# Neighbourhood attention with stationary values: two heads in two column halves of the array, and the reciprocals transposed into the bank of the products

## The chip, the cores and the metric

The kernel runs on one core of one Trainium2 chip. The metric is the device time of one execution in microseconds (us). The profile and the trace come from one further execution that the hardware profiler recorded. Engines are PE (TensorE, the matrix array; PEld is its weight load), DVE (VectorE), ACT (ScalarE), POOL (GpSimd) and SP (which issues DMAs).

## The reference

One step of a two-layer network over 128 context tokens and 512 latent tokens, 640 in all, width 1024. The change lies in layer 1, in its attention alone. Cut to that:

```python
def context_attention(q, k, v):              # the 128 context tokens, 8 heads of 64
    s = jnp.einsum('bhqd,bhkd->bhqk', qi, k) * scale
    p = jax.nn.softmax(s, axis=-1)
    return jnp.einsum('bhqk,bhkd->bhqd', p, v)

def neighbourhood_attention(q, k, v, k_ctx, v_ctx, rpb):   # 512 latent tokens on an 8 x 64 grid
    ...
    s_loc = jnp.einsum('bhrcqd,bhrcyxd->bhrcqyx', qg, k_blk) * scale + bias
    s_ctx = jnp.einsum('bhrcqd,bhld->bhrcql', qg, k_ctx) * scale
    s = jnp.concatenate([s_loc.reshape(b, h, rows, ncb, Q_COLS, n_loc), s_ctx], axis=-1)
    p = jax.nn.softmax(s, axis=-1)
    out = (jnp.einsum('bhrcqyx,bhrcyxd->bhrcqd', p_loc, v_blk)
           + jnp.einsum('bhrcql,bhld->bhrcqd', p[..., n_loc:], v_ctx))
    return out.reshape(b, h, t, dh)
```

The output of the attention, together with that of a recurrent layer (S5) on other columns, goes through one projection. Around it stand normalisations, a 4096-wide squared-ReLU MLP per layer, and in layer 0 a pooling and convolution mixer.

## The kernel before

Activations lie transposed: features on the partitions, the 640 tokens along the free dimension. Nearly all of the time is matrix products of 128 x 128 weights against 320 tokens at a time, in three products each (high part and low part of both operands), from one helper line, L304. Instructions are issued in the order in which the Python code runs; the framework adds the semaphores and hands out the buffers. Each engine works through its own queue in that order, so an instruction that waits holds up everything behind it on its engine.

Attention (`attention`, a generator) has 20 steps: 4 pairs of heads `j`, and for each the query blocks `cb` = 0 to 4 of 128 queries. Blocks 0 to 3 are latent ones and see 384 keys (256 local, 128 of the context cache); block 4 is the context block and sees 128. In step `i` the generator issues, in this order, work for four different steps:

- `scores(i + 2)`: on PE the scores of both heads, each head on its own 64 rows of the array (L1391);
- `softmax(i + 2)`: on DVE the bias is added (L1399) and the maximum taken (L1401);
- `pv(i)`: on PE the value products (L1437) into a PSUM bank `bk`, then on DVE a multiplication by the reciprocal of the softmax sum into a tile `o` in SBUF (L1440);
- `trans(i + 1)`: on DVE the reciprocal (L1413); on PE `out(i - 1)`, the transposition of the finished `o` (L1445), then the transpositions of the exponentials `P` (L1419), all into one PSUM tile `pp`; on ACT the copy of the transposed `P` to `pT` (L1422), and `keep(i - 1)`, which writes the finished output as a high part (ACT, L453) and a low part (DVE, L454), both by the helper `two`;
- `expo(i + 2)`: on ACT the exponentials of the two heads with their sums (L1408).

PSUM has two kinds of buffers: three of the tiles `pp` (two banks each, `self.ps()`), and two single banks `bk` (`self.bank()`), which are handed out in turn. A buffer's next user waits until every reader of its last content is done.

`layer1` strews other work between the steps. Before steps 0, 2, 5, 7, 10 and 12 there is a projection `qk` of 48 products (L304, some 7 us of PE) whose result ACT copies to `xq` (L1113) before it splits the next weights (`wh`, L266). After steps 8, 16, 18 and 19 there is `s5_out`, 48 smaller products of the S5 layer (L1502, L1504), which ACT copies to `yp` (L1510) and sends out by a DMA that it issues itself. After steps 6, 9, 11 and 13 ACT and DVE turn parts of the S5 state round (`s5_turn`, L1484 and L1485), and before each `qk` DVE has a piece of the S5 scan in its queue (`scan_pump`).

Elsewhere in the program one line already has the form that the change brings in: L999 (the kernel matrices of S5) loads 64 columns of weights and streams 144 columns, twice side by side, into partitions 0 to 63 and 64 to 127 of one bank.

Of the kernel before, what the change touches and what calls it, by code (L numbers as in the profile page):

```python
# [6 lines left out]
F32 = mybir.dt.float32  # L7
F32R = mybir.dt.float32r
AF = mybir.ActivationFunctionType
# [196 lines left out]
class Net:  # L206
# [1151 lines left out]
    def attention(self):  # L1358
        nc = self.nc
        todo = [(j, cb) for j in range(4) for cb in (0, 1, 2, 3, 4)]  # L1360
        N = len(todo)
        st, bms = {}, {}
        self.rel_load(0)
        self.nb = self.nm = 0
        tok = lambda cb: slice(0, 128) if cb == 4 else slice(128 + 128 * cb, 256 + 128 * cb)

        def bias_ahead():
            while self.nb < min(N, self.nm + 2):
                if todo[self.nb][1] < 4:
                    bms[self.nb] = self.att_bias(*todo[self.nb])  # L1370
                self.nb += 1

        self.bias_ahead = bias_ahead
        yield

        def scores(i):
            j, cb = todo[i]
            if cb == 0 and j < 3:
                self.rel_load(j + 1)
            pt = self.ps()  # L1380
            q, k = self.q[j % 2], self.k[j % 2]
            if cb == 4:
                ks, w = [(0, k[:, 0:128])], 128
            else:
                g = 128 + 64 * (0, 1, 3, 4)[cb]
                ks, w = [(0, k[:, g:g + 256]), (256, self.ck[:, j])], 384
            for h in range(2):
                r = slice(64 * h, 64 * (h + 1))
                for o, kk in ks:
                    kk = kk[r]  # L1390
                    nc.tensor.matmul(pt[:, h, o:o + kk.shape[-1]], q[r, tok(cb)], kk, start=True, stop=True)  # L1391
            st[i] = [pt, w]

        def softmax(i):
            j, cb = todo[i]
            pt, w = st[i]
            self.nm += 1
            if cb < 4:
                nc.vector.tensor_add(pt[:, :, 0:256], pt[:, :, 0:256], bms.pop(i))  # L1399
            sm = self.tmp.tile([128, 3, 2], F32, name="sm", tag="sm", bufs=4)  # L1400
            nc.vector.tensor_reduce(sm[:, 0], pt[:, :, 0:w], axis=AX, op=OP.max, negate=True)  # L1401
            st[i].append(sm)

        def expo(i):
            pt, w, sm = st[i]
            P = self.tmp.tile([128, 2, 384], F32, name="P", tag="pa")
            for h in range(2):
                nc.scalar.activation(P[:, h, :w], pt[:, h, :w], AF.Exp, bias=sm[:, 0, h:h + 1], accum_out=sm[:, 1, h:h + 1])  # L1408
            st[i] = [P, sm, w]

        def trans(i):
            P, sm, w = st[i]
            nc.vector.reciprocal(sm[:, 2], sm[:, 1])  # L1413
            pt = self.ps()
            if i > 1:
                out(i - 2, pt[:, 0, 384:512])
            for h in range(2):
                for b in range(w // 128):
                    nc.tensor.transpose(pt[:, h, 128 * b:128 * (b + 1)], P[:, h, 128 * b:128 * (b + 1)], self.ident)  # L1419
            pT = self.t3("pT", 768).rearrange("p (h k) -> p h k", h=2)  # L1420
            for h in range(2):
                nc.scalar.activation(pT[:, h, :w], pt[:, h, :w], AF.Copy)  # L1422
            if i > 1:
                keep(i - 2)
            st[i][0] = pT

        def pv(i):
            j, cb = todo[i]
            pT, sm, w = st[i]
            po = self.bank()  # L1430
            vt, mix = self.vt, self.mix
            vs = ([vt[:, 1], vt[:, 2], self.cv], [mix[0], mix[1], self.cv], [mix[1], mix[2], self.cv],
                  [vt[:, 3], vt[:, 4], self.cv], [vt[:, 0]])[cb]
            for h in range(2):
                hs = slice(64 * (2 * j + h), 64 * (2 * j + h + 1))
                for b, vv in enumerate(vs):
                    nc.tensor.matmul(po[:, 64 * h:64 * (h + 1)], pT[:, h, 128 * b:128 * (b + 1)], vv[:, hs],  # L1437
                                     start=b == 0, stop=b == len(vs) - 1)
            o = self.tmp.tile([128, 2, 64], F32, name="o", tag="o")
            nc.vector.tensor_mul(o, po[:, 0:128].rearrange("p (h d) -> p h d", h=2),  # L1440
                                 sm[:, 2, :, None].to_broadcast([128, 2, 64]))
            st[i] = o

        def out(i, p):
            nc.tensor.transpose(p, st[i].rearrange("p h d -> p (h d)"), self.ident)  # L1445
            st[i] = p

        def keep(i):
            j, cb = todo[i]
            self.two(st.pop(i), *(a[:, tok(cb)] for a in self.os[j]))  # L1450

        bias_ahead()
        for i in range(2):
            scores(i)
            softmax(i)
        expo(0)
        expo(1)
        yield
        trans(0)
        for i in range(N):  # L1460
            bias_ahead()
            if i + 2 < N:
                scores(i + 2)
            if i + 2 < N:
                softmax(i + 2)
            pv(i)
            if i + 1 < N:
                trans(i + 1)
            if i + 2 < N:
                expo(i + 2)  # L1470
            if i == N - 1:
                for n in (i - 1, i):
                    out(n, self.bank()[:, 0:128])
                    keep(n)
            yield

    def s5_turn(self, q):
# [116 lines left out]
```

## Time and profile before

| what | value |
|---|---|
| time of three runs, median (lowest to highest) | 1484.7 us (1480.81 to 1505.91) |
| the profiled execution: its time | 1483.03 us |
| its span in the trace | 1481.3 us |
| mean granted clock of PE over the span | 0.987 |
| PE busy, share of the span | 96% |
| DVE, ACT, POOL busy | 60%, 33%, 40% |

The span begins with the first instruction and ends with the last; 1.7 us lie outside it. Busy shares are averages over stages with different limits. The attention steps with all that is strewn between them take the stretch from 812.5 to 936.5 us of the span.

### The profile page before, as it was taken

What the parts mean: (1) busy time and instruction counts of PE and PEld (TensorE: products, weight loads), DVE (VectorE), ACT (ScalarE), POOL (GpSimd) and SP (SyncE); (2) the same over time, 40 slices, a digit from 0 to 9 for tenths busy, and PEclk for the clock granted to TensorE, in tenths of its full rate; (3) what the DMA queues carried; (4) which work ended last, traced back from release to release, by engine and by line L of the source; (5) the groups of instructions that cost most, each with busy time, mean ns of one, the idle gap of its engine ahead of it and who ended that gap; (6) DMA issues with size and microseconds to landing.
All of it is one profiled execution on the core that took longest, in us unless ns stands there. A gap on an engine that the chain in (4) does not pass through costs nothing.

```text
span 1481.3 us, 24120 instructions
## 1 busy us (share of the span) xinstructions
PE 1428.6 (96%) x9757; PEld 1397.0 (94%) x9757; DVE 882.5 (60%) x1618; ACT 484.7 (33%) x856; POOL 587.8 (40%) x429
## 2 busy tenths in 40 slices
PE   7999999999999999999989999999999999999997
PEld 7999899999999999999988888998999999999996
DVE  7899986889988888844539764427541211211213
ACT  4321234312423432433433445535322312311321
POOL 2333021326788679734324321050433333333341
PEclk9999999999999999999999999999999999999998
DMA  9245531514544545524673323521532222222211
GB/s 377 86 174 175 185 129 59 186 57 142 194 173 152 176 169 175 178 83 155 224 219 127 99 80 101 201 72 58 169 116 72 72 86 72 72 81 76 73 58 71
DMA packets 73966, 193.30 MB, mean 131 GB/s; under 512 B 15360, under 2 KB 23936, under 8 KB 73344
## 3 DMA queue, kind: packets, MB, share of 16 engines
q1 hardware_dynamic: 68976, 188.99, 37.8%
q10 hardware_dynamic: 4880, 2.78, 0.6%
q8 instruction: 77, 1.26, 0.4%
q14 instruction: 33, 0.27, 0.1%
HBM read 170.51 MB, written 22.54 MB: 130 GB/s over the span
## 4 chain that ended last, share of the span: by engine, by line
PE 73%; DVE 13%; issue 5%; ACT 3%; POOL 2%; DMA 2%; SPq 0%; ACTq 0%; DVEq 0%; POOLq 0%
PE pp L304 64%; DVE condb L335 3%; PE bk L1437 2%; DVE wl L271 1%; PE pp L1319 1%; DVE x L449 1%; PE pp L1504 1%; PE bk L1242 1%; DVE hl L443 1%; PE pp L1419 1%; ACT wh L266 1%; PE pp L1391 1%; DMA raw<-wts 1%; PE bk L999 1%; DVE pb L681 1%
## 5 line engine op out<-in xcount | busy, mean ns | idle before, releaser
L273 POOL TENSOR_TENSOR wl<-raw,wh 128x1024 fp32r<-128x1024 f32 x112 | 277.3, 2480 | 605.2 <-ACT wh L266 545.0
L304 PE MATMUL pp<-hh,wl 128*128 128x320 f32 x1472 | 360.6, 316 | 9.7 <-ACT hh L437 6.3
L304 PE MATMUL pp<-hl,wh 128*128 128x320 f32 x1472 | 355.4, 312 | 2.2 <-DVE hl L636 2.0
L304 PE MATMUL pp<-hh,wh 128*128 128x320 f32 x1472 | 354.3, 311 | 0.0
L266 ACT ACTIVATE wh<-raw 128x1024 fp32r<-128x1024 f32 x178 | 186.3, 1051 | 327.3 <-PE pp L304 234.0
L304 PE MATMUL pp<-dh,wl 128*128 128x320 f32 x1152 | 280.1, 310 | 5.6 <-DVE x L449 2.7
L304 PE MATMUL pp<-dh,wh 128*128 128x320 f32 x1152 | 278.0, 309 | 0.0
L304 PE MATMUL pp<-dl,wh 128*128 128x320 f32 x1152 | 278.0, 309 | 0.0
L304 PEld LDWEIGHTS pp<-hh,wl 128*128 128x128 f32 x1472 | 251.9, 190 | 14.1 <-ACT hh L437 7.0
L304 PEld LDWEIGHTS pp<-hl,wh 128*128 128x128 f32 x1472 | 252.9, 190 | 3.7 <-DVE hl L636 2.8
L304 PEld LDWEIGHTS pp<-hh,wh 128*128 128x128 f32 x1472 | 253.0, 190 | 0.0
L449 DVE SCALAR_TENSOR_TENSOR x<-pp,mod,x 128x128 f32<-128x128 f32 (+2 forms) x240 | 91.5, 433 | 241.6 <-PE pp L304 241.3
L304 PEld LDWEIGHTS pp<-dh,wl 128*128 128x128 f32 x1152 | 195.9, 188 | 8.8 <-issue 5.6
L304 PEld LDWEIGHTS pp<-dl,wh 128*128 128x128 f32 x1152 | 196.6, 188 | 0.3 <-DVE dl L454 0.3
L304 PEld LDWEIGHTS pp<-dh,wh 128*128 128x128 f32 x1152 | 196.5, 188 | 0.0
L335 DVE SCALAR_TENSOR_TENSOR condb<-ada,condb 128x1024 bf16<-128x1024 f32 x124 | 182.7, 1474 | 2.4
L775 DVE SCALAR_TENSOR_TENSOR pp<-pp,t 128x640 f32<-128x640 f32 x64 | 53.1, 830 | 179.9 <-ACT t L774 179.9
L774 ACT ACTIVATE t<-pp 128x640 f32<-128x640 f32 x64 | 45.1, 704 | 253.4 <-PE pp L304 238.5
L392 POOL TENSOR_TENSOR acc<-acc,sq 128x320 f32<-128x320 f32 (+1 forms) x36 | 40.0, 1112 | 129.6 <-ACT sq L391 121.4
L271 DVE TENSOR_TENSOR wl<-raw,wh 128x1024 fp32r<-128x1024 f32 x66 | 90.0, 1363 | 0.0
L391 ACT ACTIVATE sq<-x 128x320 f32<-128x320 f32 (+1 forms) x51 | 29.1, 570 | 113.4 <-DVE x L449 107.0
L777 DVE TENSOR_TENSOR dl<-pp,dh 128x640 fp32r<-128x640 f32 x64 | 52.6, 822 | 3.9 <-DVE pp L775 0.5
(249 smaller groups left out, 1601.2 us busy)
## 6 DMA issues: line engine op xcount, KB each, us to landing
raw<-wts SPq DMA_DIRECT2D x178, 512.0 KB, 3.5
ada<-ada SPq DMA_DIRECT2D x80, 512.0 KB, 4.4
spare<-ada SPq DMA_DIRECT2D x16, 512.0 KB, 3.5
est<-s5e SPq DMA_DIRECT2D x16, 256.0 KB, 4.6
fst<-s5fc SPq DMA_DIRECT2D x16, 256.0 KB, 4.5
et<-est SPq DMA_DIRECT2D x16, 256.0 KB, 3.7
ft<-fst SPq DMA_DIRECT2D x8, 512.0 KB, 4.1
x<-x SPq DMA_DIRECT2D x8, 320.0 KB, 5.2
```

Source lines behind the costliest of these rows:

```text
L266: self.nc.scalar.activation(wh, raw, AF.Copy)
L271: self.defer(lambda: self.nc.vector.tensor_sub(wl, raw, wh.bitcast(F32)))
L273: self.nc.gpsimd.tensor_sub(wl, raw, wh.bitcast(F32))
L304: self.nc.tensor.matmul(o, a[:, w], b[:, s], start=first and n == 0, stop=last and n == 2)
L335: self.nc.vector.scalar_tensor_tensor(self.junk, a, 1.0, self.condb[:, c], op0=OP.mult, op1=OP.mult, accum_out=self.mod[:, l, j, f, c:c + 1])
L391: self.nc.scalar.activation(q, self.x[f][:, s], AF.Square)
L392: (self.nc.vector if f >= last else self.nc.gpsimd).tensor_add(self.acc[:, s], self.acc[:, s], q)
L449: self.nc.vector.scalar_tensor_tensor(self.x[f][:, s], p[:, s.start - 320 * h:s.stop - 320 * h], self.mod[:, l, j, f, c:c + 1], self.x[f][ ...
L774: self.nc.scalar.activation(t, p, AF.Relu)
L775: self.nc.vector.scalar_tensor_tensor(p, p, 0.0, t, op0=OP.max, op1=OP.mult)
L777: self.defer(lambda: self.nc.vector.tensor_sub(dl, p, dh.bitcast(F32)))
L1437: nc.tensor.matmul(po[:, 64 * h:64 * (h + 1)], pT[:, h, 128 * b:128 * (b + 1)], vv[:, hs], start=b == 0, stop=b == len(vs) - 1)
```

## The change

The value products swap their operands. Before, the transposed exponentials `pT` (128 keys x 128 queries) were the weights and 64 columns of values were streamed; the result had queries on the partitions. Now 64 columns of values are the weights and the 128 columns of `pT` are streamed; the result has the head's features on the partitions, head 0 in 0 to 63 and head 1 in 64 to 127, already transposed, so `out` and its transposition are gone. The reciprocals must then lie along the free dimension: DVE spreads them over 64 columns per head into a tile `r`, PE transposes `r` into columns 256 to 383 of the bank that takes the products, ACT copies that to `rt` in SBUF, and DVE multiplies the products by `rt` into columns 128 to 255 of the same bank. `keep` reads its source there, and now stands after `expo` at the end of the step; step `i` still keeps step `i - 1`.

```diff
@@ trans(i)
             nc.vector.reciprocal(sm[:, 2], sm[:, 1])
+            r = self.tmp.tile([128, 2, 64], F32, name="r", tag="o")
+            nc.vector.tensor_copy(r, sm[:, 2, :, None].to_broadcast([128, 2, 64]))
             pt = self.ps()
-            if i > 1:
-                out(i - 2, pt[:, 0, 384:512])
...
-            if i > 1:
-                keep(i - 2)
-            st[i][0] = pT
+            st[i][:2] = pT, r
@@ pv(i)
-            for h in range(2):
-                hs = slice(64 * (2 * j + h), 64 * (2 * j + h + 1))
-                for b, vv in enumerate(vs):
-                    nc.tensor.matmul(po[:, 64 * h:64 * (h + 1)], pT[:, h, 128 * b:128 * (b + 1)], vv[:, hs],
-                                     start=b == 0, stop=b == len(vs) - 1)
-            o = self.tmp.tile([128, 2, 64], F32, name="o", tag="o")
-            nc.vector.tensor_mul(o, po[:, 0:128].rearrange("p (h d) -> p h d", h=2),
-                                 sm[:, 2, :, None].to_broadcast([128, 2, 64]))
+
+            nc.tensor.transpose(po[:, 256:384], r.rearrange("p h d -> p (h d)"), self.ident)
+            rt = self.tmp.tile([128, 128], F32, name="rt", tag="rt")
+            nc.scalar.activation(rt, po[:, 256:384], AF.Copy)
+            for b, vv in enumerate(vs):
+                for h in range(2):
+                    hs = slice(64 * h, 64 * (h + 1))
+                    nc.tensor.matmul(po[hs, 0:128], vv[:, 128 * j + 64 * h:128 * j + 64 * (h + 1)],
+                                     pT[:, h, 128 * b:128 * (b + 1)], start=b == 0, stop=b == len(vs) - 1)
+            o = po[:, 128:256]
+            nc.vector.tensor_mul(o, po[:, 0:128], rt)
             st[i] = o
-
-        def out(i, p):
-            nc.tensor.transpose(p, st[i].rearrange("p h d -> p (h d)"), self.ident)
-            st[i] = p
@@ the loop over the steps
                 trans(i + 1)
             if i + 2 < N:
                 expo(i + 2)
+            if i:
+                keep(i - 1)
             if i == N - 1:
-                for n in (i - 1, i):
-                    out(n, self.bank()[:, 0:128])
-                    keep(n)
+                keep(i)
```

On PE, step 6 (the second of the two steps between two projections) stood before as follows; a row is the line, the operation, out<-in by tile names and the shape of the result, with the engines that it waits for in brackets.

```order
L1391 MATMUL pp<-attc,xq 128x128
L1437 MATMUL bk<-mix_8004,pT 128x64 [waits Activation_49]
L1437 MATMUL bk<-mix_8005,pT 128x64
L1437 MATMUL bk<-attc,pT 128x64
L1437 MATMUL bk<-mix_8004,pT 128x64 [waits Activation_49]
L1437 MATMUL bk<-mix_8005,pT 128x64
L1437 MATMUL bk<-attc,pT 128x64
L1445 MATMUL pp<-const,o 128x128 [waits DVE_49]
L1419 MATMUL pp<-const,P 128x128 [waits Activation_49]
```

The same place now:

```order
L1391 MATMUL pp<-attc,xq 128x128
L1433 MATMUL bk<-const,r 128x128 [waits DVE_49]
L1439 MATMUL bk<-pT,mix_8004 64x128 [waits Activation_49]
L1439 MATMUL bk<-pT,mix_8004 64x128
L1439 MATMUL bk<-pT,mix_8005 64x128 x2
L1439 MATMUL bk<-pT,attc 64x128 x2
L1419 MATMUL pp<-const,P 128x128 [waits PE_49]
```

The transposition of the reciprocals has moved in ahead of the value products, with a wait for DVE, and the transposition of `o` behind them is gone. In the built program the DVE instruction that L1433 waits for in step `i` is the low part (L454) of step `i - 2`, the last reader of that bank's former content, and the ACT instruction that the first L1439 waits for is the copy to `rt` out of the same bank (L1435 of the changed file).

On ACT, between two projections (steps 5 and 6), there stood before:

```order
L1113 ACTIVATE xq<-pp 128x640
L266 ACTIVATE wh<-raw 128x1024
L1422 ACTIVATE pT<-pp 128x384 x2
L453 ACTIVATE o_8031<-pp 128x128
L1408 ACTIVATE P,sm<-pp,sm 128x384 x2
L1422 ACTIVATE pT<-pp 128x384 x2
L453 ACTIVATE o_8031<-pp 128x128
L1408 ACTIVATE P,sm<-pp,sm 128x384 x2
```

And now:

```order
L1113 ACTIVATE xq<-pp 128x640
L266 ACTIVATE wh<-raw 128x1024
L1435 ACTIVATE rt<-bk 128x128
L1422 ACTIVATE pT<-pp 128x384 x2
L1408 ACTIVATE P,sm<-pp,sm 128x384 x2
L453 ACTIVATE o_8031<-bk 128x128
L1435 ACTIVATE rt<-bk 128x128
L1422 ACTIVATE pT<-pp 128x384 x2
L1408 ACTIVATE P,sm<-pp,sm 128x384 x2
L453 ACTIVATE o_8031<-bk 128x128
```

The copy to `rt` stands behind the weight split and ahead of the copies to `pT`; the high part of the finished output (L453) has moved behind the exponentials.

## Rows read from the trace of the kernel before

**Rows 1.** Windows: busy us (instructions) per engine, PEclk, DMA share, GB/s; the attention.
```profile
812.50:936.50 124.00, 115.08 (x895) 107.23 (x893) 72.86 (x162) 57.04 (x163) 27.05 (x30) 0.97 0.34 101
```

**Rows 2.** Timeline of PE, steps 5 and 6: start us, us, engine, line, operation.
```profile
846.79 0.71 PE L1391 MATMUL pp<-xq 64*128 64x256 f32 x4
...
847.65 0.66 PE L1437 MATMUL bk<-vt,pT 128*128 128x64 f32 x4
...
849.16 0.82 PE L1419 MATMUL pp<-const,P 128*128 128x128 f32 x6
849.91 0.71 PE L1391 MATMUL pp<-xq 64*128 64x256 f32 x4
...
852.84 0.54 PE L304 MATMUL pp<-hh,wl 128*128 128x320 f32 x2
```

**Rows 3.** Timeline of ACT and DVE in the same stretch.
```profile
846.90 0.70 ACT L1113 ACTIVATE xq<-pp 128x640 f32<-128x640 f32 x1 [4.89 <-PE pp L304]
847.50 1.05 ACT L266 ACTIVATE wh<-raw 128x1024 fp32r<-128x1024 f32 x1
...
850.01 0.87 ACT L1422 ACTIVATE pT<-pp 128x384 f32<-128x384 f32 x2 [1.46 <-PE pp L1419]
...
850.77 0.28 ACT L453 ACTIVATE o<-pp 128x128 fp32r<-128x128 f32 x1
850.93 0.59 ACT L1408 ACTIVATE P<-pp,sm 128x384 f32<-128x384 f32 x1
851.09 0.29 DVE L454 TENSOR_TENSOR o<-pp,o 128x128 fp32r<-128x128 f32 x1 [1.28 <-ACT o L453]
...
851.95 0.23 ACT L1408 ACTIVATION_READ_ACCUMULATOR P<-pp,sm 128x1 f32 x1
```

**Rows 4.** Timeline of PE at one block of L999, and the projection behind it.
```profile
378.30 0.71 PE L999 MATMUL bk<-s5f,bd 128*64 128x144 f32 x8
378.94 0.56 PE L304 MATMUL pp<-hh,wl 128*128 128x320 f32 x2
...
379.63 0.46 PE L304 MATMUL pp<-hl,wh 128*128 128x320 f32 x2
```

**Rows 5.** Timeline around ACT's copy `yp` behind step 8.
```profile
870.89 0.70 ACT L1510 ACTIVATE yp<-pp 128x640 f32<-128x640 f32 x1 [3.52 <-PE pp L1504]
871.63 0.38 ACTq L1511 DMA_DIRECT2D yds<-yp  x1
```

**Rows 6.** Timeline of ACT behind step 13: `s5_turn`.
```profile
905.60 1.57 ACT L1484 ACTIVATE tn<-S 64x128 f32<-64x128 f32 x4
```

**Rows 7.** Timeline of DVE and PE around steps 0 and 1.
```profile
815.26 0.66 PE L1437 MATMUL bk<-vt,pT 128*128 128x64 f32 x4 [1.08 <-ACT pT L1422]
...
819.85 0.15 DVE L1413 RECIPROCAL sm<-sm 128x2 f32<-128x2 f32 x1
...
821.93 0.30 PE L1445 MATMUL pp<-const,o 128*128 128x128 f32 x1 [2.12 <-DVE sm L1413]
...
823.27 0.54 PE L304 MATMUL pp<-hh,wl 128*128 128x320 f32 x2
...
832.02 0.49 PE L1391 MATMUL pp<-xq 64*128 64x128 f32 x4
```

**Rows 8.** Timeline of DVE and PE around step 11.
```profile
887.38 0.96 DVE L1401 TENSOR_REDUCE sm<-pp 128x2 f32<-128x768 f32 x1
...
888.53 0.27 DVE L454 TENSOR_TENSOR o<-pp,o 128x128 fp32r<-128x128 f32 x1
...
888.85 0.48 PE L1445 MATMUL pp<-const,o 128*128 128x128 f32 x1 [3.34 <-DVE o L454]
...
890.29 0.88 PE L304 MATMUL pp<-hh,wl 128*128 128x320 f32 x2
```

**Rows 9.** Windows as in Rows 1: steps 0 and 1 with the projection behind; steps 12 to 16.
```profile
812.50:832.00 19.50, 16.12 (x109) 14.70 (x107) 15.94 (x42) 6.78 (x17) 4.98 (x5) 0.91 0.39 112
...
898.30:914.30 16.00, 14.64 (x122) 12.38 (x121) 9.95 (x24) 11.23 (x34) 6.38 (x7) 1.00 0.36 124
```

More of the change, by code (lines that the diff above doesn't have):

```diff
@@ L1422, in trans @@
                 nc.scalar.activation(pT[:, h, :w], pt[:, h, :w], AF.Copy)
-            if i > 1:
-                keep(i - 2)
-            st[i][0] = pT
+            st[i][:2] = pT, r
         def pv(i):
             j, cb = todo[i]
-            pT, sm, w = st[i]
+            pT, r, w = st[i]
             po = self.bank()
```

## The prediction

> **What bounds the kernel now.** I read the table first, then the windows, then the timelines of single engines. PE is busy for 96% of the span, and in the attention for 115.1 of 124.0 us at a mean clock of 0.97 [rows 1]: here too PE sets the pace, so PE time saved is time saved, and any new wait of PE is time lost. The timeline shows how well a step is overlapped. From scores to scores a full step takes PE 849.91 - 846.79 = 3.12 us, and no row of it waits [rows 2]: scores 0.86, values and the transposition of `o` together 849.16 - 847.65 = 1.51, transpositions of `P` 0.75. ACT and DVE run beside that with slack, because PE asks them early for what it needs late: the value products need only `pT`, whose copies run from 850.01 to 850.88 [rows 3], beside the scores that start at 849.91.
>
> **What the change takes off PE.** Twelve products and one transposition go (1.51); a transposition of the reciprocals and six pairs of products come. The pairs have a model in L999: four pairs of 144 columns take 378.94 - 378.30 = 0.64, entry and exit of the split array included [rows 4]. Scaled to six pairs of 128 columns that is 0.64 x 6/4 x 128/144 = 0.85. With the transposition and its change of array mode (about 0.2 by the spacing of the six in 0.75) a step would take 1.05 in place of 1.51. Sixteen steps have three blocks of keys; the four context steps (one block) gain about nothing. PE work alone falls by 16 x 0.46, some 7 to 8 us.
>
> **What it adds: two waits.** First, L1433 waits for the low part of step i - 2, since step i uses the bank that step i - 2 finishes in. Before, that bank was free as soon as DVE had multiplied. Now ACT must write the high part first, and that now stands behind the exponentials of step i + 1. Second, the products wait for ACT's copy of the transposed reciprocals out of their own bank. Queued behind both waits on PE are the transpositions of the next `P` and all projections.
>
> The loop that this closes, for a step right behind another, from one first value product to the next, each part from [rows 2, 3] unless named: products 0.85; transpositions until ACT starts on them 850.01 - 849.16 = 0.85; `pT` until the next ACT operation starts 0.76; two exponentials with their sums 852.18 - 850.93 = 1.25; high part 0.28 and low part 0.29, with 0.03 and 0.04 to start them; PE's restart 0.06 (888.80 to 888.85, [rows 8]); transposition of the reciprocals 0.30 [rows 7]; start and copy 0.05 + 0.28 (as L453, a PSUM read of the same size); products restart 0.05 (both starts put as the restart above). Sum 5.1 us, against 3.12: **2.0 us lost per full step**. The multiplication and the spread of the reciprocals (0.2 to 0.3 each, by the 0.29 of a DVE operation of this size) lie beside the loop and cost nothing, as long as DVE has been reached in time.
>
> Which steps stand right behind another: 1, 3, 4, 6, 8, 11, 13 to 16 and 18 (two or three between projections; fillers behind 8, 16, 18, 19). Step 6 loses 2.0. Where the exponentials in the loop are those of a context block (3, 8, 13, 18), they are a third as long and the loop is about 0.5 shorter: 1.5 each, 1.7 for 18, which has no scores to cover. Steps 4 and 15, with a context block between, 1.5 each. Step 14 stands behind the four copies of `s5_turn`, 1.57 on ACT [rows 6], of which about 0.9 is covered: 1.5 + 0.7 = 2.2. Before step 16 PE waits already (16.00 us hold only 14.64 busy, [rows 9]), so only 0.7 is new. Together 2.0 + 3 x 1.5 + 1.7 + 2 x 1.5 + 2.2 + 0.7 = **14.1**.
>
> Steps behind a projection (2, 5, 7, 12; 10 below) have the bank free, but ACT first copies the projection and splits weights: 846.90 to 848.55, 1.76 after the scores began [rows 3]. Then the copy to `rt`, and the first product starts at about 2.15 in place of 847.65 - 846.79 = 0.86: 1.3 lost for step 5, and 1.75 for the three whose scores are those of a context block, half as long (0.49, [rows 7]). Together **6.6**. Behind `s5_out` ACT first has `yp` and its DMA issue, 0.70 + 0.38 [rows 5]: start at 1.65 after PE is free; 0.8, 1.2 and 1.65 lost at steps 9, 17, 19, together **3.7**.
>
> At the last step of each group the shorter products count in full, since no wait follows them: 1.51 - 0.85 at steps 6, 8, 16, 18, 0.2 to 0.35 at the context steps 4 and 9, and 0.8 at 19, where two transpositions at the end go. **Gain 4.0.**
>
> **Step 11** already waits for DVE, which comes from the S5 scan: the maximum ends at 888.34, PE restarts at 888.85 and reaches the projection at 890.29 [rows 8]. Now PE resumes only after exponentials, high and low part (888.34 + 1.3 + 0.3 + 0.35 = 890.3), then transposition and copy (0.7), products 0.85, transpositions 0.6: 892.4, **2.1 lost**. **Steps 0 and 1:** the products of step 0 started at 815.26 without the reciprocals, whose instruction stands on DVE behind the scan until 819.85 [rows 7]. Now they wait for it: 820.0 + 0.25 spread + 0.7 = 821.0. Then 0.85 + 0.85 + 0.76 to the exponentials of step 2, their 1.25, the copy to `rt` behind them on ACT 0.35: step 1 at 825.1, transpositions at 825.95, projection at 826.55 in place of 823.27: **3.3 lost**.
>
> At full clock that is 14.1 + 6.6 + 3.7 - 4.0 + 2.1 + 3.3 = **25.8 us**.
>
> **The clock.** The granted clock of PE fell to half (1.2 of 2.4 GHz) twice in the attention: behind the wait of 2.12 us that ends at 821.93 (0.91 over that window, [rows 7, 9]) and behind the one of 3.34 that ends at 888.85, where the transposition takes 0.48 in place of 0.30 [rows 7, 8]. Steps 12 to 16, with some 1.4 us of waits in all, kept 1.00 [rows 9]. A fall costs about 1.5: the projection from 823.27 to 832.02 took 8.75, against 48 products at (379.63 - 378.94)/4 = 0.15, 7.2 [rows 4, 7]. The nine steps above now wait 1.4 to 1.9 for the bank and 0.4 for the copy: between the stretch that kept the clock and the one that lost it. Bounds are 0 falls and 9; I take 5, since 1.8 to 2.3 is nearest to 2.12: **7.5 us**.
>
> **Sum:** 25.8 + 7.5 = 33.3 on the profiled execution's 1483.0, which is 1.7 below the median of the runs: **1516 us**.
>
> **A rule that bears on it.** L999's pairs start side by side: eight products in 0.64 [rows 4]. The Trainium skill's page TensorEngine Tiling, section Performance Considerations, advises just this swap where the streamed side has 64 columns or fewer, for up to twice the speed; by it alone the sum would be the 7 to 8 us less of the first rival. The order shows the products behind ACT's copy out of their own bank, and no row of before has a bank shared in that way. The Trainium skill's page PSUM — Partial Sum Buffer, section Terms (PSUM bank), calls a TensorE write and a ScalarE read in the same bank and quadrant at once an error, so that wait would not be an accident of the framework; no run here shows more of it.
>
> **Rivals.** *The waits are hidden and only the PE work counts:* 1483 - 8 = 1475, faster within 2%. It decides where at least 5.1 us of other PE work lie between two value products. The projections (7.2 us) and `s5_out` do that, or nearly, at eight steps of twenty; against it, the ACT queue, which has its own work exactly there [rows 3, 5]. 4%. *Only one wait bites*, say because the low part is done earlier than I think: the loop is then 3.1 as before, and the entries, steps 0, 1 and 11 remain, some 12 us: 1495. For it: DVE has gaps of over 1 us before L454 [rows 3]; against it, these gaps are themselves waits for ACT. 8%. *The loop is right, and the clock does not fall more often than before:* 1509. For it: steps 12 to 16 kept their clock. 33%. *The forecast,* 1516, with 4 to 6 more falls: 43%. *The clock stays low through whole groups*, so that products and transpositions of the nine steps and half of the projections behind take twice their time: 25.8 + 9 x 1.5 + 5 = 44, 1528 and above: 12%.
>
> **Range and chances.** A change of 2% is about what a measurement of this kernel can tell from none; it is 1514.4 against the median. The range 1495 to 1532 leaves out the first rival, half of the second and the upper end of the last. Some 60% of the forecast, a quarter of the clock-neutral case and all of the last lie above 1514: 0.26 + 0.08 + 0.12, and something for what I may have priced low in steps 0 and 1: 0.5 slower, 0.49 within, 0.01 faster.
>
> **What would show it.** In the changed profile: value products of a step right behind another start 5 us after those of the step before, with PE waiting over 1 us for L454 ahead of the transposition of reciprocals and 0.4 for the copy behind it; six pairs of products in 0.8 to 0.9; step 0's products not before 821; more stretches of PEclk under 1 in the attention; and nothing changed before 812 or after the projection that follows. I am wrong if PE does not wait at L1433, if the pairs do not run side by side, or if the loss comes from another stage.

## The result, and the profile after

The changed kernel takes 1536.2 us (median of 4 runs, 1532.2 to 1541.1) where the kernel before takes 1484.2: a ratio of 1.036 (95% interval 1.033 to 1.038), 3.6% slower. The forecast was 1516, with a range to 1532. The profiled execution took 1533.3, 50.2 more than that of before. Over all runs told below the kernel before itself spread from 1480 to 1513, since some of its runs were granted a clock of only 0.96 to 0.97; the ratios leave most of these out, but three of the ten runs of before behind the ratios of `e1_o_sbuf` to `e4_fill` are such, so those four ratios are some 0.4% low.

The page of the changed kernel: the span, the row of PE's busy time, and from the 40 slices PE's busy share and PEclk.

```profile
span 1531.5 us, 24180 instructions
...
PE 1452.4 (95%) x9757; PEld 1411.5 (92%) x9757; DVE 887.2 (58%) x1638; ACT 488.6 (32%) x876; POOL 588.7 (38%) x429
...
PE   7999999999999999999897797899999999999997
...
PEclk9999999999999999999999977699999999999998
```

PE's busy time rises although its work should have fallen by 7 to 8 us, and PEclk drops to 7, 7 and 6 in three slices of the attention: products that run at the low clock count as busy for longer.

To see where, both kernels' attention is cut at the starts of its projections (columns as in [rows 1]): steps 0 and 1, 2 to 4, 5 and 6, 7 to 9, 10 and 11, and 12 to 19 up to the projection behind the attention. Each window opens with a projection. Before:

```profile
805.40:823.30 17.90, 14.52 (x109) 13.28 (x108) 17.42 (x34) 9.49 (x21) 11.72 (x9) 1.00 0.58 164
823.30:839.60 16.30, 16.30 (x116) 15.18 (x114) 9.82 (x28) 7.28 (x23) 5.42 (x6) 0.90 0.22 54
839.60:852.80 13.20, 13.20 (x103) 12.54 (x102) 9.62 (x19) 5.97 (x16) 3.10 (x6) 1.00 0.22 82
852.80:872.80 20.00, 20.00 (x165) 19.13 (x163) 11.68 (x26) 9.91 (x28) 2.27 (x4) 1.00 0.26 77
872.80:890.30 17.50, 14.16 (x105) 13.23 (x103) 14.02 (x22) 7.90 (x20) 4.89 (x5) 0.96 0.35 102
890.30:936.50 46.20, 43.99 (x358) 40.99 (x356) 17.26 (x46) 21.36 (x66) 6.38 (x7) 0.98 0.35 111
```

After:

```profile
807.70:830.00 22.30, 14.90 (x110) 13.03 (x109) 18.47 (x39) 9.88 (x23) 11.79 (x9) 0.85 0.47 132
830.00:848.90 18.90, 14.24 (x116) 12.06 (x114) 11.40 (x30) 8.00 (x26) 6.17 (x7) 1.00 0.34 102
848.90:865.20 16.30, 13.37 (x105) 11.82 (x104) 10.22 (x23) 6.41 (x18) 3.03 (x5) 0.96 0.01 2
865.20:895.90 30.70, 27.26 (x164) 24.68 (x162) 13.22 (x28) 10.42 (x31) 2.76 (x4) 0.72 0.26 73
895.90:913.40 17.50, 14.44 (x104) 12.82 (x103) 12.10 (x23) 8.13 (x22) 4.36 (x3) 0.89 0.18 62
913.40:985.10 71.70, 58.59 (x356) 51.07 (x355) 19.56 (x50) 23.44 (x74) 6.43 (x7) 0.69 0.24 76
```

The attention takes 177.4 us in place of 131.1: 46.3 of the 50.2. (Its first projection also starts 2.3 later, where nothing was changed, and 1.6 comes behind it.) Where PEclk is 1.00, steps 2 to 4, the loss is 2.6 (before's window holds a fall of its own clock, 0.90); the two windows with 0.72 and 0.69 lose 10.7 and 25.5.

PE at steps 2 and 3 of the changed kernel, at full clock, against [rows 2] (in square brackets the idle time ahead and what ended it):

```profile
839.18 0.66 PE L1439 MATMUL bk<-pT,mix 128*64 128x128 f32 x8 [1.22 <-ACT rt L1435]
839.67 0.39 PE L1439 MATMUL bk<-pT,attc 128*64 128x128 f32 x4
839.99 0.87 PE L1419 MATMUL pp<-const,P 128*128 128x128 f32 x6
...
841.32 0.40 PE L1391 MATMUL pp<-attc,xq 64*128 64x128 f32 x4
843.01 0.33 PE L1433 MATMUL bk<-const,r 128*128 128x128 f32 x1 [1.29 <-DVE o L454]
843.76 0.66 PE L1439 MATMUL bk<-pT,vt 128*64 128x128 f32 x8 [0.43 <-ACT rt L1435]
```

From 839.18 to 839.99 the six pairs take 0.81. The next value products start 4.58 behind them; PE waits 1.29 for the low part and 0.43 for the copy to `rt`. Step 2, behind a projection, waits 1.22 for the copy alone. Over the whole attention (us in total, times, longest):

```profile
PE bk L1439 <- ACT rt L1435: 14.5, 20, 1.4
PE bk L1433 <- DVE o L454: 14.2, 10, 2.2
PE bk L1433 <- DVE r L1415: 5.9, 1, 5.9
```

The stretches at half clock, as windows; their sum:

```profile
880.80:897.90 17.10, 16.73 (x80) 15.54 (x78) 3.07 (x10) 4.36 (x14) 1.87 (x3) 0.50 0.31 86
...
928.60:942.30 13.70, 10.43 (x56) 6.99 (x52) 6.72 (x18) 6.12 (x21) 2.07 (x4) 0.50 0.05 20
...
959.40:986.70 27.30, 25.48 (x122) 24.21 (x123) 1.76 (x8) 3.17 (x10) 0.00 (x0) 0.50 0.25 75
sum 75.10, PE 66.24 PEld 58.54 DVE 19.39 ACT 17.20 POOL 6.43; mean PE 9.46 PEld 8.36 DVE 2.77 ACT 2.46 POOL 0.92
```

There are seven such stretches, 75.1 us in all (the four that aren't shown are 3.4 to 6.8 long). Before had two, from 823.9 to 827.4 and from 888.8 to 892.2, 6.9 us in all. The first of those shown holds a whole `s5_out`: behind step 8 and its two waits, PE at the half level (1.2 of 2.4 GHz) without one wait more:

```profile
879.28 0.33 PE L1433 MATMUL bk<-const,r 128*128 128x128 f32 x1 [1.29 <-DVE o L454]
880.04 0.66 PE L1439 MATMUL bk<-pT,vt 128*64 128x128 f32 x8 [0.43 <-ACT rt L1435]
...
881.33 0.56 PE L1499 MATMUL pp<-up,at 128*128 128x80 f32 x2
...
890.63 1.06 PE L1501 MATMUL pp<-S,ft 128*128 128x80 f32 x4
891.62 1.23 PE L1391 MATMUL pp<-xq 64*128 64x256 f32 x4
```

It takes 891.62 - 881.33 = 10.3 us; at full clock it is 5.4 (868.72 to 874.14 in the run `e3_both` below). Three of the four `s5_out` run like that. Behind step 16 it went otherwise: the level had fallen at 945.7, and it came back inside `s5_out`, 0.8 us after its start:

```profile
945.70:949.10 3.40, 3.40 (x22) 3.07 (x23) 1.27 (x4) 0.51 (x2) 0.00 (x0) 0.50 0.00 0
...
948.35 0.56 PE L1499 MATMUL pp<-up,at 128*128 128x80 f32 x2
```

### The profile page after: what moved, and what is told of

Same layout as the page of the kernel before. It is cut to its first block, busy times and chain, and to the rows that moved or that the text cites. A ratio compares the mean times of both kernels' runs of the same rounds, so it can differ in the third digit from the quotient of the medians.

```text
span 1531.5 us, 24180 instructions
## 1 busy us (share of the span) xinstructions
PE 1452.4 (95%) x9757; PEld 1411.5 (92%) x9757; DVE 887.2 (58%) x1638; ACT 488.6 (32%) x876; POOL 588.7 (38%) x429
## 4 chain that ended last, share of the span: by engine, by line
PE 70%; DVE 16%; ACT 5%; issue 5%; POOL 2%; DMA 1%; ACTq 0%; SPq 0%; DVEq 0%; POOLq 0%
PE pp L304 61%; DVE condb L335 4%; PE pp L1501 2%; DVE wl L271 1%; PE bk L1439 1%; PE pp L1419 1%; DVE x L449 1%; ACT wh L266 1%; PE bk L1242 1%; DVE hl L443 1%; PE pp L1499 1%; DMA raw<-wts 1%; ACT P L1408 1%; DVE up L1268 1%; DVE S L1270 1%
## 5 line engine op out<-in xcount | busy, mean ns | idle before, releaser
L273 POOL TENSOR_TENSOR wl<-raw,wh 128x1024 fp32r<-128x1024 f32 x112 | 278.1, 2488 | 637.3 <-ACT wh L266 577.0
```

What stands on the lines that cost most here:

```text
L273: self.nc.gpsimd.tensor_sub(wl, raw, wh.bitcast(F32))
```

## The experiments

**Theory A:** the two waits cost about what was forecast (25.8), and the rest is the clock, which falls behind them and was priced too low. Rivals: the pairs themselves pull the clock down (B); one of the two waits does it alone (C: the bank, D: the copy); the low clock costs little, since PE would wait at those places anyway (E).

### Each wait by itself

`e1_o_sbuf`, the wait for the bank removed:

```diff
-            o = po[:, 128:256]
+            o = self.tmp.tile([128, 128], F32, name="o", tag="oo")
```

> The changed kernel with one line altered: the product of step i goes to an SBUF tile instead of into the bank of its value products, so the bank is free as soon as DVE has multiplied, as it was before the change. The wait for the bank is gone, the wait for the copy of the transposed reciprocals stays. Theory A (both waits close a loop through the same ACT queue: the copy to rt stands behind the exponentials of the step after, too): PE no longer waits ahead of the transposition of the reciprocals for DVE's low part, but longer behind it for the copy, and value products of a step right behind another start 4.3 to 4.5 us apart, in place of 4.6 to 5.0; the entries behind projections and s5_out are as they were. Some 6 us at full clock and a part of what the clock takes: 1515 to 1528. Rival C (the bank alone is what holds PE): the steps come back to about 3.1, 1495 to 1500. Rival D (the copy alone holds it): 1533 to 1540, no change.

Measured: 1508.2 (ratio 1.011, 1.004 to 1.019), between theory A's number and C's. PE's waits:

```profile
PE bk L1439 <- ACT rt L1435: 21.0, 20, 2.5
```

No wait for the low part is left, and the one for the copy grew from 14.5 to 21.0 (that for the spread `r` from 5.9 to 9.7). Value products of neighbouring steps start 3.5 to 4.1 apart, so the remaining loop is shorter than I had put it (4.3 to 4.5), but C's 3.1 is not reached.

`e2_rt_apart`, the wait for the copy removed:

```diff
 in trans(i), ahead of the transpositions of P:
+            if i:
+                nc.tensor.transpose(pt[:, 1, 384:512], r of step i - 1, self.ident)
 and behind the copies to pT:
+                nc.scalar.activation(rt, pt[:, 1, 384:512], AF.Copy)
+                o = po[:, 128:256]                  # po of step i - 1
+                nc.vector.tensor_mul(o, po[:, 0:128], rt)
```

> The changed kernel with the other wait removed: the reciprocals of step i are transposed ahead of the transpositions of P of step i + 1 into that step's pp tile, and copied to rt behind pT; the multiplication follows there, still into the bank of the value products, which the high and low part read. The products no longer wait for a copy; the wait for the bank stays. Theory A: value products of a step right behind another 4.2 to 4.7 us apart, all of the wait ahead of the first value product and for the low part of two steps before; the entries behind a projection or s5_out, and step 0, lose their wait for the copy: 13 to 17 us less at full clock, and about half of what the clock takes: 1500 to 1515. Rival C (the bank alone): 1528 to 1540. Rival D (the copy alone): about 1485, steps of 3 us.

Measured: 1510.0 (1.015, 1.005 to 1.024), in theory A's range. The whole wait now stands ahead of the value products:

```profile
PE bk L1439 <- DVE o L454: 21.7, 10, 5.8
```

Either wait alone holds the loop at 3.5 to 4.5 us; C and D fall.

`e6_keep_first`, the changed kernel with one call moved:

```diff
             pv(i)
+            if i:
+                keep(i - 1)
             if i + 1 < N:
                 trans(i + 1)
             if i + 2 < N:
                 expo(i + 2)
-            if i:
-                keep(i - 1)
```

> The changed kernel with one line moved: the high and low part of step i - 1 are issued ahead of the transposition of P of step i + 1, so on ACT they stand ahead of pT and the exponentials instead of behind them; bank, tile and copy as in the changed kernel. If the place of these two lines is what makes the wait for the bank, the transposition of the reciprocals no longer waits for the low part, the wait for the copy stays as with the product in SBUF (value products 3.5 to 4.1 apart), and the time is that run's: 1500 to 1512. If the bank is held by something else (the low part on DVE behind the maximum of step i + 2, say), PE still waits for L454 and the time is 1515 to 1535.

Measured: 1508.9 (1.016, 1.010 to 1.021), as `e1_o_sbuf`, and no wait for L454 at the bank. So the place of the high and low part behind the exponentials is what made the wait for the bank; one moved call gives back 27 of the 52 us. A good part of that is the clock: in the profiled execution (1498.9; the others reach 1515.9, with granted clocks from 0.986 down to 0.972) PE is at the half level for 13.7 us of the attention, in place of 75.1.

### Both waits removed

`e3_both`: the edits of `e1_o_sbuf` and `e2_rt_apart` together.

> Both waits removed: reciprocals transposed into the pp tile of the next step, the product in an SBUF tile; the value products stay as pairs in two halves of the array's columns. Theory A (the waits cost the time, and the clock falls behind waits): a step takes PE 2.7 to 2.9 us in place of 3.12, no PE wait of over 0.2 us in the steps behind projections and right behind others, the granted clock falls as seldom as before the change (twice), and the time is 1472 to 1482. Rival B (the pairs themselves pull the granted clock down, or disturb what runs beside them): PEclk below 1 for more than 20 us of the attention though the waits are gone, time 1495 and above.

Measured: 1488.2 (0.998, 0.995 to 1.002): as before the change, not below it. The mechanism is as expected, the time isn't. PE at step 5 (L1444 transposes the reciprocals):

```profile
850.38 0.71 PE L1391 MATMUL pp<-xq 64*128 64x256 f32 x4
...
851.24 0.66 PE L1439 MATMUL bk<-pT,vt 128*64 128x128 f32 x8
...
852.04 0.33 PE L1444 MATMUL pp<-const,r 128*128 128x128 f32 x1
...
852.96 0.49 PE L1391 MATMUL pp<-xq 64*128 64x256 f32 x2
```

Scores to scores 2.58 in place of 3.12 [rows 2], without a wait: the pairs do take 0.54 off a step. Rival B falls: all pairs are there, and the clock falls twice, as before, though the first time for longer (10.3 and 3.4 us, where before had 3.5 and 3.4). But PE waits elsewhere:

```profile
PE pp L1444 <- DVE r L1415: 11.5, 7, 4.3
```

These waits are for DVE. What holds DVE? DVE at step 6 of this kernel:

```profile
854.14 0.29 DVE L1452 TENSOR_TENSOR o<-bk,rt 128x128 f32<-128x128 f32 x1 [0.20 <-ACT rt L1450]
855.46 0.29 DVE L454 TENSOR_TENSOR o<-o,o 128x128 fp32r<-128x128 f32 x1 [1.03 <-ACT o L453]
```

It stands 1.03 us at the low part, for a high part behind two exponentials. Four runs followed that.

`e7_bcast`, the spread of the reciprocals off DVE:

```diff
-            r = self.tmp.tile([128, 2, 64], F32, name="r", tag="o")
-            nc.vector.tensor_copy(r, sm[:, 2, :, None].to_broadcast([128, 2, 64]))
+            r = sm[:, 2, :, None].to_broadcast([128, 2, 64])
...
-            nc.tensor.transpose(p, r.rearrange("p h d -> p (h d)"), self.ident)
+            for h in range(2):
+                nc.tensor.matmul(p[64 * h:64 * (h + 1)], r[:, h], self.ident, start=True, stop=True)
```

> The kernel with both waits removed, and without DVE's spread of the reciprocals: each head's reciprocals go to TensorE as a column read 64 times, two products by the identity in the two halves of the columns in place of one transposition. DVE loses 20 copies of 0.23, 4.5 us, and the chain from the sum of the exponentials to the transposition loses one link. If DVE is what the kernel with both waits removed now waits for (its transposition of reciprocals waits 1.2 to 3 us for the spread at steps 1, 9 and 12): 1478 to 1485, 2 to 6 below it. If those waits are for the maximum ahead of it, which the exponentials need as well: no change, 1484 to 1490.

Measured: 1488.0 (1.003, 0.999 to 1.006), no change. Of the 11.5 us of waits 9.9 are left, now for the reciprocal (L1413): PE waits for what stands ahead of the spread.

`e10_both_keep_first`: `e3_both` with the call moved as in `e6_keep_first`.

> The kernel with both waits removed, with the high and low part of step i - 1 issued ahead of the transpositions of P of step i + 1. In that kernel DVE is the engine that PE waits for (11.5 us, for the spread of the reciprocals), and DVE itself waits about 1 us in each step at the low part, for ACT's high part that stands behind two exponentials. If that wait on DVE is where the gain of the pairs went: DVE no longer idles ahead of the low part, PE's waits for the spread fall from 11.5 to under 7, and the time is 1478 to 1484. If DVE is bound by its work (the scan and the maxima) and not by this wait: 1484 to 1489, as without it.

Measured: 1489.7 (1.002, 0.999 to 1.004). In steps 5 to 11 DVE no longer idles ahead of L454, but the low part takes 0.64 on average in place of 0.29, and PE's wait for `r` is 13.8 in place of 11.5. The wait on DVE was not where the gain went. The trace also shows what stretches the low part:

```profile
851.64 1.39 POOL L1355 TENSOR_TENSOR bm<-attc,const 128x256 f32<-128x256 f32 x2 [7.65 <-DVE pp L1399]
852.47 0.71 DVE L454 TENSOR_TENSOR o<-o,o 128x128 fp32r<-128x128 f32 x1
...
866.09 0.28 DVE L454 TENSOR_TENSOR o<-o,o 128x128 fp32r<-128x128 f32 x1
```

GpSimd works on the biases (L1355) or on a weight split (L273) beside every low part that takes 0.68 or more (eleven, two of them 2.35), and beside none of the nine that take 0.28 or 0.29. In the kernel before the low part reads one operand from PSUM (`o<-pp,o`), and there it takes 0.27 to 0.29 beside GpSimd as well (four times).

`e12_bcast_keep`: both edits, `e7_bcast` with the call moved.

> The same without GpSimd: high and low part early, on ACT and DVE, reciprocals as a broadcast column. Between the two runs beside it: 1475 to 1484 if DVE's work sets the pace, and within 2 of the run with the transposition of spread reciprocals if only the wait for the high part counted.

`e11_pool_low`: that, and the low part on GpSimd.

```diff
-            self.two(st.pop(i), *(a[:, tok(cb)] for a in self.os[j]))
+            o, (dh, dl) = st.pop(i), (a[:, tok(cb)] for a in self.os[j])
+            nc.scalar.activation(dh, o, AF.Copy)
+            nc.gpsimd.tensor_sub(dl, o, dh.bitcast(F32))
```

> As the run beside it (high part early), with the reciprocals read as a broadcast column by TensorE instead of spread by DVE, and with the low part computed on GpSimd instead of DVE. DVE loses 20 x (0.23 + 0.29) = 10 us of work in the attention. If DVE's work sets the pace where PE waits: 1473 to 1481, below the kernel before by 0.3 to 0.6%. If what is left of PE's waits is the S5 scan's (steps 0, 1 and 11, 7 to 8 us) and GpSimd is slower at the low part or slows DVE beside it: 1480 to 1487.

Measured: 1485.4 (0.999, 0.996 to 1.001) for `e12_bcast_keep`, which fits neither of its cases, and 1484.2 (0.999, 0.997 to 1.001) for `e11_pool_low`, the second of its two: the lowest medians with pairs, and no difference from before that the runs can tell. DVE and PE of `e11_pool_low`, at steps 0 and 11 (L1444: reciprocals) and behind the `s5_out` between them:

```profile
822.31 0.69 PE L1444 MATMUL pp<-const,sm 128*64 128x128 f32 x4 [3.83 <-DVE sm L1413]
...
874.18 0.70 DVE L1399 TENSOR_TENSOR pp<-pp,bm 128x512 f32<-128x512 f32 x1 [5.28 <-PE pp L1391]
...
884.47 3.69 DVE L1304 TENSOR_TENSOR S<-S,up 128x504 f32<-128x504 f32 x2
...
890.81 0.15 DVE L1413 RECIPROCAL sm<-sm 128x2 f32<-128x2 f32 x1
...
891.11 0.44 PE L1444 MATMUL pp<-const,sm 128*64 128x128 f32 x4 [4.11 <-DVE sm L1413]
```

Where the gain of the pairs goes, window by window (cut at the projections, us):

| steps | before | `e3_both` | `e11_pool_low` |
|---|---|---|---|
| 0, 1 | 17.9 | 21.0 | 20.4 |
| 2 to 4 | 16.3 | 15.6 | 14.4 |
| 5, 6 | 13.2 | 12.4 | 12.6 |
| 7 to 9 | 20.0 | 20.5 | 20.0 |
| 10, 11 | 17.5 | 17.2 | 17.6 |
| 12 to 19 | 46.2 | 46.8 | 46.6 |

Steps 0 and 1 lose 2.5 to 3.1. The reciprocals of step 0 stand on DVE behind the scan; PE needs them one step earlier in its queue than it needed the first `o` before, and waits 3.83 for them, with 0.64 ahead of the products (`e3_both`: 2.36 and 1.74), where before it waited 2.12 and 1.08 [rows 7]. Steps 2 to 6 give back 1.5 and 2.5; part of this is the clock, whose first fall lies in the window of steps 2 to 4 before and in that of steps 0 and 1 here. Step 11's reciprocal then comes 16.6 us behind the start of the biases that follow `s5_out` (874.18), in the kernel before 16.7 (871.77 to 888.45): this stretch holds the turn of the state on ACT and the scan on DVE, and PE, which arrives a little earlier, waits 4.11 in place of 3.34 [rows 8]. It is not the whole way up to step 11 that DVE sets: ahead of those biases DVE itself stood idle for 5.3 us for PE's scores, in both kernels. In steps 12 to 19 PE waits again for DVE and ACT (4.1 us in `e3_both`, before 2.2). These are windows of one execution each, and not all of the difference is accounted for; no run removed the wait of steps 0 and 1 or that of step 11.

`e8_heads_apart`, `e3_both` with the products of one head behind those of the other:

```diff
-            for b, vv in enumerate(vs):
-                for h in range(2):
+            for h in range(2):
+                for b, vv in enumerate(vs):
```

> The kernel with both waits removed, with the loops over heads and blocks swapped: the three products of one head run one after another and then those of the other, so that no two neighbours but one pair lie in different halves of the columns. It tells what running side by side is worth. If neighbours in different halves start together and others don't: value products of a step with three blocks in 1.2 to 1.5 in place of 0.81, scores to scores 3.0 to 3.2 in place of 2.58, and 2 to 8 us more in all, as far as PE sets the pace. If the order doesn't matter (the gain comes from products of half the columns): 0.8 as now and no change.

Measured: 1488.5 (one run), with six products in 1.07 (850.31 to 851.38) in place of 0.80 (851.24 to 852.04 in `e3_both`). Alternating the halves is worth 0.27 a step, and this too doesn't show in the time of that one run.

### The clock by itself

Three kernels keep both waits and let PE multiply the identity by itself in them. `e4_fill`, ahead of the scores:

```diff
 in scores(i), i > 2:
+            for _ in range(8):
+                nc.tensor.matmul(pt[:, 0, 0:128], self.ident, self.ident, start=True, stop=True)
 in pv(i), behind the copy to rt: the same three times, into the tile of the next transpositions
```

> The changed kernel with both of its waits left, and PE kept at work in them: from step 3 on, eight products of the identity by itself into the scores' tile ahead of the scores, and three into the next P transpositions' tile between the transposition of the reciprocals and the value products, all overwritten later. Eight at the 0.12 us of such a product fill 1.0 us of the wait for the bank, three 0.36 of that for the copy. Theory A: steps right behind each other keep the 4.6 to 5.0 us of the changed kernel (at most 0.4 more), but the clock holds at 1.0 except at steps 0, 1 and perhaps 11, where other waits are not filled; what is gained is what the low clock cost: 1505 to 1516. Rival B (the pairs pull the clock down, whatever PE does between): the low stretches stay, 1533 to 1545. Rival E (the low clock costs little, since PE would wait at those places anyway): the clock is up and the time within 8 us of 1536.

Measured: 1525.0 (1.023, 1.015 to 1.031). The clock is up (the whole execution 0.989, against 0.963), so B falls here too; but the time agrees with no theory. The filling delays: steps 2 to 4 with their projection take 21.3, where the changed kernel needs 18.9 at full clock.

`e5_fill_free`, into the other bank:

```diff
+            fill(i, 6)        # products into columns 384:512 of the bank of step i - 1
             nc.tensor.transpose(po[:, 256:384], r.rearrange("p h d -> p (h d)"), self.ident)
             rt = self.tmp.tile([128, 128], F32, name="rt", tag="rt")
             nc.scalar.activation(rt, po[:, 256:384], AF.Copy)
+            fill(i, 3)
```

> The changed kernel with both waits left and PE kept at work in them, as in the run with filling before, but where the filling should delay nobody: from step 1 on, six products of the identity by itself into unused columns of the other bank (that of step i - 1) behind the scores and ahead of the transposition of the reciprocals, and three more between that transposition and the value products: 0.73 and 0.36 us at 0.12 us each. The run before filled ahead of the scores, and a stretch that ran at full clock in the changed kernel (three steps and a projection, 18.9 us) took 21.3 there, so part of its time was the filling's own. Theory A as forecast (waits cost 25.8 at full clock, the rest of the 52 is the clock): 1505 to 1512, that stretch within 0.7 of 18.9, low clock for under 20 us of the attention. Rival E (the low clock costs little, since PE would wait there anyway): 1518 to 1530 with the clock up all the same. Rival F (it takes more than this filling to hold the clock): low for more than 40 us, 1525 and above.

Measured: 1518.5 (1.024, 1.019 to 1.028), by its number rival E's case. But the test stretch took 20.2 in place of 18.9, not within the 0.7 asked for: such a product is two instructions of 0.12, so the filling was twice as long as meant, and behind projections it put off the transposition of the reciprocals.

`e9_fill_fit`, the same with counts fitted to the waits:

```diff
+        ENTRY = {1: 4, 2: 5, 5: 3, 7: 5, 9: 2, 10: 4, 12: 5, 17: 3, 19: 4}
...
-            fill(i, 6)
+            fill(i, 0 if i in ENTRY else 3 if i == 14 else 5)
...
-            fill(i, 3)
+            fill(i, ENTRY.get(i, 2))
```

> Filling once more, now sized by the waits that the changed kernel's trace shows. In the two runs before, each product of the identity took two instructions of 0.12 us, so that nine products were 2.2 us and not 1.1; behind projections and s5_out, where the only wait is the one for the copy, six of them stood ahead of the transposition of the reciprocals and put it off by 0.7 to 0.8. Now steps 1, 2, 5, 7, 9, 10, 12, 17 and 19 have none ahead of that transposition and two to five behind it, the others five ahead (three at step 14) and two behind. Theory A (waits cost about 26 at full clock, the clock the other 24): the clock holds from step 2 on, the steps start as far apart as where the changed kernel ran at full clock, and the time is 1506 to 1513. Rival E (the run with free filling was right as it stood, at 1518: waits 35, clock 17): 1515 to 1521. If the clock falls again somewhere, the time is 1513 to 1528 and the low stretches tell by how much.

Measured: 1511.8 (1.017, 1.014 to 1.019), in theory A's range and below E's. The same six windows:

```profile
809.20:832.30 23.10, 16.65 (x117) 14.63 (x117) 18.63 (x39) 9.99 (x23) 11.67 (x9) 0.85 0.44 127
832.30:851.40 19.10, 18.85 (x155) 16.52 (x153) 11.47 (x31) 8.02 (x26) 6.30 (x7) 1.00 0.35 101
851.40:867.10 15.70, 15.08 (x125) 13.55 (x123) 9.99 (x21) 6.42 (x18) 2.90 (x5) 1.00 0.01 2
867.10:890.20 23.10, 22.76 (x192) 20.66 (x190) 12.71 (x26) 10.44 (x31) 2.20 (x4) 1.00 0.28 76
890.20:910.00 19.80, 16.79 (x128) 15.31 (x126) 14.56 (x27) 8.24 (x22) 4.64 (x4) 0.91 0.26 80
910.00:965.70 55.70, 51.28 (x446) 45.85 (x445) 19.71 (x51) 23.49 (x74) 6.43 (x7) 1.00 0.32 96
```

The clock falls twice, at steps 0, 1 and 11, as before the change (for 6.9 and 3.4 us). Steps 2 to 4 take 19.1 against the changed kernel's 18.9, both at 1.00: the filling costs 0.2 in three steps. At step 11 it costs some 0.8, since the bank is free at 906.54 and the filling runs to 907.33. Apart from that this is the changed kernel with its waits at about before's clock. It is 24.5 us below the changed kernel by the medians, 21.3 by the profiled executions: that is the clock.

## Why the prediction failed

**The waits: right.** The attention of `e9_fill_fit` is longer than before's by 156.5 - 131.1 = 25.4; the sum at full clock said 25.8. Some 1.0 of the 25.4 is the filling's own, as said above. Window by window, forecast and measured (before's window from that of `e9_fill_fit`):

| steps | forecast terms | sum | measured |
|---|---|---|---|
| 0, 1 | 3.3 | 3.3 | 5.2 |
| 2 to 4 | 1.75 + 1.5 + 1.5, less 0.2 | 4.6 | 2.8 |
| 5, 6 | 1.3 + 2.0, less 0.66 | 2.6 | 2.5 |
| 7 to 9 | 1.75 + 1.5 + 0.8, less 0.66 and 0.35 | 3.0 | 3.1 |
| 10, 11 | 2.1 | 2.1 | 2.3 |
| 12 to 19 | 1.75 + 5.9 + 1.2 + 1.7 + 1.65, less 2.1 | 10.1 | 9.5 |

In the first two rows before's own fall of the clock lies in the window of steps 2 to 4 (its projection took 8.75, [rows 7]) and that of `e9_fill_fit` in the one ahead; together they are 7.9 and 8.0. The loop of a full step was put at 5.1 and took 5.0 at full clock (858.11 to 863.12 in the changed kernel; 4.2 to 4.6 where a context block stands in it, put about 0.5 shorter), the pairs at 0.85 and took 0.81, the wait for the copy at 0.4 and was 0.43, step 0's products at 821.0 and came at 823.3 (820.9 when counted from the projection ahead).

**The clock: the term that failed.** Its count was right, five falls more (seven in place of two), and its price wrong: 1.5 each, 7.5 in all. It measured 20.9 in the attention (177.4 - 156.5), 4.2 each. The count was luck: it was chosen by the size of the waits, and the waits ahead of steps 3 and 4, which kept the clock, are the same 1.29 and 0.43 as those of steps 8 and 13, which lost it. The 1.5 came from one row, a projection in which the level came back soon [rows 7]; its working is wrong on paper, as (379.63 - 378.94)/4 is 0.17 and not 0.15, but the 7.2 is right (before step 5 the projection runs from 839.57 to 846.79). Two of the falls here stood ahead of an `s5_out` instead, and the level stayed low through it and up to the projections behind: 4.9 at the `s5_out` shown above, and about as much at the two behind steps 18 and 19. By windows, the changed kernel less `e9_fill_fit`: 7.6 at steps 7 to 9, 16.0 at steps 12 to 19, 0.6 at 5 and 6, and -2.3 at 10 and 11. The last rival of the prediction, a low clock through whole groups, was the right mechanism, with a chance of 12%. Its own price (44 us, so 1528 at the least) was too low as well: it doubled the nine steps and half the projections and left `s5_out` out.

**Step 11** counted 2.1 for a wait that the changed kernel doesn't have: its window is 17.5 before and after, since PE arrives so late that the scan is done. `e9_fill_fit`, which arrives earlier, waits 2.98 for it. Step 10 was left without a term.

**"PE time saved is time saved": wrong here.** `e3_both` and the four runs behind it have the gain on PE and not in the time: it shows in steps 5 and 6, and is lost to waits for DVE and ACT at steps 0, 1, 11 and behind, so the first rival's 8 us weren't there to be had. The rule of the Trainium skill's page TensorEngine Tiling, section Performance Considerations, held for PE's work (2.58 in place of 3.12 a step) and told nothing of the time.

**The rest of the difference** of forecast and measurement (33.3 against 50.2): 13.4 by the clock in the attention, 1.6 behind it, into which the last stretch at half clock runs on, and 2.3 by the later start of the attention, where the two kernels don't differ (in the other profiled executions it starts between 803.1 and 810.5), less 0.4 for the waits. The sum was also added to the profiled 1483.0 and not to the median, which makes it 1.7 low.

What stays open: why the level stayed low through three `s5_out` and came back in the fourth. No run changed that.

## What to carry to other kernels

Price a fall of the clock by the work that follows it, not by the stretch in which it was last seen to recover: list what stands behind each wait, and take as the worst case the lower level for all of it, up to work in which a trace has shown the level coming back. A copy out of the bank that the next products need, and a release that stands behind long operations on the same queue, close a loop between two engines; look where in the queue the releasing instruction stands, since moving that one call gave back 27 of 52 us. And before counting saved time of the busiest engine, look for the waits at which it meets another engine's chain, and for an operand that it will now need earlier: here both took the saving back.

## What the hardware showed that was not expected

- At the half level, `s5_out` (products of 128x80) ran low to its end, 10.3 us, in a stretch with PE busy for 16.7 of 17.1 us; behind step 16 the level came back 0.8 us into it. Steps 2 to 4, where PE was busy for only 14.2 of 18.9 us with waits of 1.2 to 1.3, kept the full clock.
- Products whose neighbours lie in different halves of the columns take 0.80 for six (`e3_both`) where the same six, one half behind the other, take 1.07 (`e8_heads_apart`).
- A product of the identity by itself in f32 is two instructions of 0.12 us (`e5_fill_free`: twelve from 836.93 to 838.38 for six products), the transposition of a tile of the same size one.
- A DVE operation of 128x128 with both operands in SBUF takes 0.68 to 0.71, or 2.35, where it meets work on GpSimd, and 0.28 alone (`e10_both_keep_first`); with one operand in PSUM it takes 0.27 to 0.29 beside it as well (L454 of the kernel before). The scan meets it too: in the kernel before, the two operations of the scan that start at 882.05 take 3.56 beside a weight split on GpSimd (881.96 to 884.34), elsewhere 1.40. That is in the stretch that step 11 waits for, and moving that split was not tried.
